# Three constant products of a recurrence: plain float32, or two float32r products of split parts

## The chip, the cores and the metric

The kernel runs on one core of a Trainium2 chip. The metric is the device time of one execution in microseconds; a kernel's time is the median of its runs. A profile of one execution stands beside the times: it gives every instruction's start and length on each engine.

## The reference, cut to what matters

One layer of a hybrid encoder block works on 2048 tokens of width 1024: a combined projection, chunked attention, an RWKV-7 recurrence with 8 heads of 64, a gated merge, and a feed-forward part. The change lies in the recurrence, in what is computed of r, k and v before the scan:

```python
kk = heads(k * k_k)
kk = kk / jnp.maximum(jnp.sqrt(jnp.sum(kk * kk, axis=-1, keepdims=True)), 1e-12)
...
mu = jnp.mean(y, axis=-1, keepdims=True)
yn = (y - mu) * lax.rsqrt(var + GN_EPS)
...
bonus = jnp.sum(r_h * k_h * r_k.astype(jnp.float32), axis=-1, keepdims=True) * v_h
```

Three of its sums run over the 64 channels of a head: the sum of squares of kk, the mean that is taken from the output (the kernel takes it from v ahead of the scan, since the output is linear in v), and the bonus sum.

## The kernel before, in words

The 2048 tokens go through in four groups of 512 (`for g in range(self.NG)` in `run`). In each group `phase_rwkv` handles four pairs of heads (128 channels on the partitions), then `phase_attention` and `phase_merge` follow; after the four groups comes the feed-forward part. `rwkv_pre` (line 418 on) runs once for each pair and group, so 16 times in all. The text calls the four pairs of a group pair 0 to 3. Pairs 0 and 1 are prepared in the open; pairs 2 and 3 are prepared while the matrix inverse and the recurrence of pairs 0 and 1 are under way.

Nearly all of TensorE's work is dense projections. `dense` (line 117) forms a block of 128 output columns for 512 tokens out of 24 products of 128x128 by 128x512: the float32 operands are split into a float32r high part (ScalarE's cast, line 80) and a low part (VectorE's subtraction, line 81), and `mm3` (line 83) issues high by high, high by low and low by high. The tile is called psd. `self.mm` is the last product of the latest dense block.

`rwkv_pre` forms r, k and v of the pair by dense blocks and `mix` (token shift: ScalarE lines 372 and 375, GpSimd's column copies of `carry` lines 373 and 374, VectorE line 376). Then come, all in plain float32 on TensorE:

- sums of squares: sq is k squared on ScalarE (line 461); ps_ss takes four products, sq's 128 tokens as the stationary side and the 128x2 constant bones2 as the moving side (line 464). n2t on VectorE is the inverse (lines 466, 467), and GpSimd spreads it into n2 (line 474).
- centred values: ps_v takes four products of v's 128 tokens with the 128x128 constant cmat (line 516); ScalarE copies them into SV (lines 520, 521).
- bonus: r times r_k times k on VectorE (line 502); ps_bonus is one product of the constant bones with the 128x512 tile r (line 525); VectorE multiplies it by v (line 526) and GpSimd's queue stores it (line 527).

BK (lines 496, 499) holds the decayed keys that ps_bk (line 536) and ps_A (line 557) read. mN (line 505) is a masked copy of n2 that is read when ps_A is moved out (line 573). AR, tk, ta, Ei are further operands of the same pair.

The order on each engine is set by a list scheduler when the kernel is built: it goes by program order and by its own estimates of when inputs are ready. `between()` places a dense block of the output gates, or a piece of the running recurrence, at marked points of `rwkv_pre` (the tables `GATES` and `STEPS`). `tc.issue_after(x)` holds an instruction behind x on its engine. Once built, the order on an engine is fixed: an instruction that isn't ready holds up all behind it. PSUM tiles of tag "a" come from a pool of two buffers; tags "BK" and "mN" have one buffer each.

Of the kernel before, what the change touches and what calls it, by code (L numbers as in the profile page):

```python
# [17 lines left out]
P = 128  # L18
# [5 lines left out]
G = 512  # L24
GT = G // P
C = 64
NC = G // C
# [27 lines left out]
class Block:  # L55
# [109 lines left out]
    def constants(self, ctx, mixing):  # L165
        tc, nc, a = self.tc, self.nc, self.a
        keep = ctx.enter_context(tc.tile_pool(name="const", bufs=1))
        cp = mixing.enter_context(tc.tile_pool(name="mconst", bufs=1, side="right"))
# [4 lines left out]
        self.g2c = keep.tile([P, 2 * KB], F32, name="g2c")  # L173
        self.nhalf = keep.tile([P, 8], F32, name="nhalf")
        nc.vector.memset(self.nhalf, -0.5)
        self.bones = cp.tile([P, P], F32, name="bones")
        nc.vector.memset(self.bones, 0.0)
        for h in range(2):
            nc.vector.memset(self.bones[h * C : h * C + C, h * C : h * C + C], 1.0)
        self.bones2 = cp.tile([P, 2], F32, name="bones2")  # L180
        nc.vector.memset(self.bones2, 0.0)
        for h in range(2):
            nc.vector.memset(self.bones2[h * C : h * C + C, h : h + 1], 1.0)

        self.id64 = cp.tile([P, C], F32, name="id64")
        for h in range(2):
            nc.vector.tensor_copy(self.id64[h * C : h * C + C], self.ident[h * C : h * C + C, h * C : h * C + C])
        self.cmat = cp.tile([P, P], F32, name="cmat")
        nc.vector.scalar_tensor_tensor(
            self.cmat, self.bones, -1.0 / C, self.ident, op0=ALU.mult, op1=ALU.add  # L190
        )
# [30 lines left out]
        with tc.tile_pool(name="setup", bufs=1, side="right") as sp, \  # L222
# [18 lines left out]
            ps = pp.tile([P, nrow], F32, name="ps_rows")  # L241
# [4 lines left out]
            for par in range(2):  # L246
                r = slice(par * C, par * C + C)
# [132 lines left out]
    def tmp(self, name, shape=(P, G)):  # L380
        return self.tp.tile(list(shape), F32, tag="t", name=name)

    def lora_wa(self, g):

        nc, lp = self.nc, self.lp
        rows = [slice(0, C), slice(C, P)]
        lw = self.tmp("lw")
        self.mix(g, 12, lw)
        nc.scalar.activation(lw[0:C], lw[0:C], AF.Tanh)

        self.lo = []
# [27 lines left out]
    def rwkv_pre(self, g, p, rp, NA, between, pools):  # L419
        nc = self.nc  # L420
        pc = slice(p * P, (p + 1) * P)
        col = slice(p, p + 1)
        R = {}
        r = self.tmp("r")
# [3 lines left out]
        ps = self.lora(0, p)  # L428
# [5 lines left out]
        ps = self.lora(1, p)  # L434
        ta = self.tmp("ta")
        nc.scalar.activation(ta, ps, AF.Tanh, scale=0.5, bias=self.ha0[:, col])
        v = self.tmp("v")
# [22 lines left out]
        sq = self.tmp("sq")  # L460
        nc.scalar.activation(sq, k, AF.Square, scale=self.kk[:, col])
        pss = self.pa.tile([P, GT, 2], F32, tag="a", name="ps_ss")
        for t in range(GT):
            nc.tensor.matmul(pss[:, t], sq[:, t * P : (t + 1) * P], self.bones2, start=True, stop=True)
        n2t = self.tp.tile([P, GT, 2], F32, tag="n2t", bufs=2, name="n2t")
        nc.vector.tensor_scalar(n2t, pss, 1e-24, None, ALU.max)
        nc.vector.reciprocal(n2t, n2t)
# [10 lines left out]
        BK = self.tp.tile([P, NC, 2, C], F32, tag="BK", bufs=1, name="BK")  # L478
# [21 lines left out]
        between()  # L500

        nc.vector.scalar_tensor_tensor(r, r, self.rk[:, col], tk, op0=ALU.mult, op1=ALU.mult)
        mN = self.tp.tile([P, 2, NC, C], F32, tag="mN", bufs=1, name="mN")
        for par in range(2):
            nc.vector.tensor_tensor(
# [2 lines left out]
                n2[:, :, par, None].to_broadcast((P, NC, C)),  # L508
                ALU.mult,
            )  # L510
        between()

        SV = rp.tile([P, NC, 2, C], F32, tag="SV", name="SV")
        psv = self.pa.tile([P, GT, P], F32, tag="a", name="ps_v")
        for t in range(GT):
            nc.tensor.matmul(psv[:, t], v[:, t * P : (t + 1) * P], self.cmat, start=True, stop=True)
        SVv = SV.rearrange("p (t h) e c -> p h t e c", h=2)
        for h in range(2):
            src = psv[h * C : h * C + C]
            nc.scalar.copy(SVv[C:P, h, :, 0], src[:, :, 0:C])  # L520
            nc.scalar.copy(SVv[0:C, h, :, 1], src[:, :, C:P])
        R["SV"] = SV

        psb = self.pa.tile([P, G], F32, tag="a", name="ps_bonus")
        nc.tensor.matmul(psb, self.bones, r, start=True, stop=True)
        nc.vector.tensor_tensor(r, psb, v, ALU.mult)
        nc.gpsimd.dma_start(self.bvd[p], r)

        between()

# [104 lines left out]
    def rwkv_trans(self, p, R):  # L635

        nc, xp = self.nc, self.xp
        AR, SV, XT, BR = (R[x] for x in ("AR", "SV", "XT", "BR"))
        rows = [slice(0, C), slice(C, P)]
# [18 lines left out]
        for h, cs in enumerate(halves):  # L658
# [1044 lines left out]
```

## Time and profile before

| what | value |
|---|---|
| time, median of 3 runs | 3239.71 us (3233.46, 3239.71, 3240.22) |
| span of the profiled execution | 3233.6 us, 49175 instructions |
| the same execution's own time | the page prints none; the runs lie 0.1 us below to 6.6 us above its span |
| TensorE products, weight loads | busy 3189.0 us (99%), 2568.5 us (79%) |
| VectorE, ScalarE, GpSimd | 2259.7 us (70%), 1572.6 us (49%), 392.5 us (12%) |
| dense products psd, three kinds | 1344 each, 533 to 542 us busy each |
| recurrence stage of the second group, 500 to 760 us | TensorE busy 256.71 of 260 us |

A matmul's busy time includes its filling and draining, which overlap with the next one's: the cost of a product is read from the distance between starts. A plain float32 product appears in the profile as two records, each with its own weight load, a float32r product as one. A row of the timeline gives the start, the length, the engine (PEld is the weight load), the line, the operation, the tiles as out<-in, the shape, and in brackets the idle time ahead of it and what ended it.

### The profile page before, as it was taken

The numbers are of one execution on the slowest core, as the hardware profiler recorded it, in microseconds if no ns is written. First come the engines' busy times: TensorE is split into PE (matmuls) and PEld (weight loads), VectorE is DVE, ScalarE is ACT, GpSimd is POOL, SyncE is SP. The second block draws the span as 40 slices with busy tenths as digits, with TensorE's granted clock in tenths as the row PEclk, the third lists the DMA queues.
The fourth block names the chain that finished last, engine by engine and source line by source line (L and its number), as shares of the span: only waits on it lengthen the run. The fifth ranks groups of instructions, "written<-read, shape, count | busy, mean of one in ns | idle before, by whom it ended". The sixth has DMA issues, their size and how long they took to land. (4 is left out here: it accounts for less than half of the span.)

```text
span 3233.6 us, 49175 instructions
## 1 busy us (share of the span) xinstructions
PE 3189.0 (99%) x18945; PEld 2568.5 (79%) x18945; DVE 2259.7 (70%) x3782; ACT 1572.6 (49%) x2551; POOL 392.5 (12%) x757
## 2 busy tenths in 40 slices
PE   8999999999999999999999999999999999999999
PEld 6777788777778777778777778878888888888887
DVE  6784556775676774576774666777778988766788
ACT  4435534444655435645434635467543454454333
POOL 2111002111021111022111000033000121100001
PEclk9999999999999999999999999999999999999999
DMA  5224343234264224354224257577546474453443
GB/s 163 91 83 151 105 145 117 73 109 168 94 241 137 79 102 149 110 206 166 85 85 151 92 182 280 185 248 254 185 169 221 161 268 177 175 169 137 158 161 130
DMA packets 166163, 498.34 MB, mean 154 GB/s; under 512 B 18141, under 2 KB 26529, under 8 KB 160553
## 3 DMA queue, kind: packets, MB, share of 16 engines
q1 hardware_dynamic: 107000, 358.33, 33.0%
q0 software_dynamic: 22688, 77.61, 6.3%
q10 hardware_dynamic: 36240, 59.26, 5.0%
q8 instruction: 149, 2.44, 0.3%
q14 instruction: 86, 0.70, 0.1%
HBM read 366.13 MB, written 132.15 MB: 154 GB/s over the span
## 5 line engine op out<-in xcount | busy, mean ns | idle before, releaser
L89 PE MATMUL psd<-hh,wlo 128*128 128x512 f32 x1344 | 534.3, 398 | 10.0 <-DVE wlo L81 10.0
L89 PE MATMUL psd<-hh,whi 128*128 128x512 f32 x1344 | 541.9, 403 | 0.4
L89 PE MATMUL psd<-hl,whi 128*128 128x512 f32 x1344 | 532.8, 396 | 0.0
L80 ACT CAST whi<-wraw 128x1024 fp32r<-128x1024 f32 x232 | 243.7, 1050 | 497.6 <-PE psd L89 355.5
L89 PE MATMUL ps_dn<-fop,fop 128*128 128x512 f32 x2016 | 457.3, 389 | 0.0
L89 PEld LDWEIGHTS ps_dn<-fop,fop 128*128 128x128 f32 x2016 | 378.5, 188 | 78.5
L81 DVE TENSOR_TENSOR wlo<-wraw,whi 128x1024 fp32r<-128x1024 f32 x232 | 282.7, 1220 | 148.5 <-ACT whi L80 147.1
L89 PEld LDWEIGHTS psd<-hh,wlo 128*128 128x128 f32 x1344 | 253.5, 189 | 68.9 <-DVE wlo L81 14.7
L89 PEld LDWEIGHTS psd<-hh,whi 128*128 128x128 f32 x1344 | 253.3, 188 | 57.1 <-issue 2.6
L89 PEld LDWEIGHTS psd<-hl,whi 128*128 128x128 f32 x1344 | 253.7, 189 | 46.3 <-issue 0.7
L80 ACT CAST fop<-ar 128x1024 fp32r<-128x1024 f32 x84 | 87.8, 1050 | 212.2 <-PE ps_dn L89 172.8
L89 PE MATMUL ps_dn<-fop 128*128 128x512 f32 x768 | 175.6, 390 | 0.3 <-DVE fop L81 0.3
L89 PEld LDWEIGHTS ps_dn<-fop 128*128 128x128 f32 x768 | 143.9, 188 | 31.4 <-DVE fop L81 0.7
L1441 DVE TENSOR_TENSOR y<-y,ps_dn 128x512 f32<-128x512 f32 x168 | 109.2, 682 | 43.5 <-PE ps_dn L89 42.7
L81 DVE TENSOR_TENSOR fop<-ar,fop 128x1024 fp32r<-128x1024 f32 x84 | 102.3, 1220 | 45.4 <-ACT fop L80 45.4
L932 DVE CUSTOM_DVE_ANT_0 sc<-bias,ps_s 128x640 f32<-128x640 f32 (+4 forms) x128 | 94.1, 735 | 56.2 <-PE ps_s L926 53.7
L937 ACT ACTIVATE sc<-sc,mn 128x640 f32<-128x640 f32 (+4 forms) x128 | 97.8, 764 | 34.9 <-DVE mn L932 33.1
L1326 POOL DMA_DIRECT2D sd<-slots x96 | 53.0, 552 | 454.1 <-DVE slots L1325 450.2
L1059 PE MATMUL ps_o<-wlo,mh 128*128 128x512 f32 x256 | 101.1, 395 | 3.6 <-DVE wlo L81 3.6
L1059 PE MATMUL ps_o<-whi,mh 128*128 128x512 f32 x256 | 101.5, 400 | 0.5 <-ACT whi L80 0.5
L89 PE MATMUL ps_p<-yh,wlo 128*128 128x512 f32 x256 | 100.9, 394 | 0.0
L1059 PE MATMUL ps_o<-whi,ml 128*128 128x512 f32 x256 | 100.9, 394 | 0.0
(381 smaller groups left out, 6817.8 us busy)
## 6 DMA issues: line engine op xcount, KB each, us to landing
wraw<-in_w_in_dram SPq DMA_DIRECT2D x168, 512.0 KB
ar<-sd SPq DMA_DIRECT2D x42, 1024.0 KB
wraw<-in_w_up_dram SPq DMA_DIRECT2D x82, 512.0 KB
sd<-slots POOLq DMA_DIRECT2D x96, 256.0 KB, 5.0
qb<-in_w_down_dram SPq DMA_DIRECT2D x24, 1024.0 KB
gd<-gate ACTq DMA_DIRECT2D x64, 256.0 KB
wraw<-in_w_out_dram SPq DMA_DIRECT2D x32, 512.0 KB
sd<-slots ACTq DMA_DIRECT2D x60, 256.0 KB
```

The costliest lines, as they stand in the source:

```text
L80: self.cast = self.nc.scalar.copy(hi, src).ins
L81: self.parted = self.nc.vector.tensor_tensor(lo, src, hi.bitcast(F32), ALU.subtract).ins
L89: mm = nc.tensor.matmul(ps, l, r, start=start and n == 0, stop=stop and n == last).ins
L932: nc.vector.tensor_tensor_reduce(sc[:, 0:n], bias[:, s0:640], pss[:, c0 : c0 + n], 1.0, 3.0e38, ALU.add, ALU.min, mn,)
L937: nc.scalar.activation(sc[:, 0:n], sc[:, 0:n], AF.Exp, scale=-1.0, bias=mn, accum_out=sm)
L1059: nc.tensor.matmul(ps[t], l[:, k, ts], r[:, k % 2], start=k == 0 and j == 0, stop=k == KB - 1 and j == 2)
L1326: nc.gpsimd.dma_start(place(i, "s3" if o == "a21" else o), R[o])
L1441: self.add = nc.vector.tensor_tensor(dst, dst, ps, ALU.add).ins
```

## The change

The constants become float32r tiles. They are exact in that form: zeros, ones, and multiples of 1/64. A new helper, `parts`, splits a 128x512 float32 tile into a float32r high part (a ScalarE copy) and a low part (a GpSimd subtraction, which reads the tile and the high part). `by_token` issues, for each of the four blocks of 128 tokens, the low part's product and then the high part's, accumulated in PSUM. The three sums are taken this way: ps_ss and ps_v by `by_token`, ps_bonus by two products of 128x512. Each of these products is held behind `self.mm`.

No memory is added: the parts of sq use the buffer of BK, and the parts of v, then those of r, use the buffer of mN. So BK is now written after ps_ss has read the parts, parts of r come after ps_v, and mN is formed after the bonus. The two `between()` calls near the bonus keep their count: one moves ahead of ps_v and mN moves behind the bonus.

```diff
@@ -173,19 +173,18 @@
-        self.bones = cp.tile([P, P], F32, name="bones")
+        self.sums = cp.tile([P, P], F32R, name="sums")
+        self.bones = self.sums.bitcast(F32)
...
-        self.bones2 = cp.tile([P, 2], F32, name="bones2")
-        nc.vector.memset(self.bones2, 0.0)
-        for h in range(2):
-            nc.vector.memset(self.bones2[h * C : h * C + C, h : h + 1], 1.0)
+        self.sums2 = cp.tile([P, 2], F32R, name="sums2")
+        nc.vector.tensor_copy(self.sums2, self.bones[:, 0 : 2 * C : C])
...
-        self.cmat = cp.tile([P, P], F32, name="cmat")
+        self.cmat = cp.tile([P, P], F32R, name="cmat")
@@ -380,6 +379,20 @@
+    def parts(self, src, tag):
+
+        both = self.tp.tile([P, 2, G], F32R, tag=tag, bufs=1, name="parts")
+        self.nc.scalar.copy(both[:, 0], src)
+        self.nc.gpsimd.tensor_tensor(both[:, 1], src, both[:, 0].bitcast(F32), ALU.subtract)
+        return both
+
+    def by_token(self, ps, both, mat):
+
+        for t in range(GT):
+            for i in (1, 0):
+                with self.tied(self.mm):
+                    self.nc.tensor.matmul(ps[:, t], both[:, i, t * P : (t + 1) * P], mat, start=i == 1, stop=i == 0)
+
@@ -460,8 +473,7 @@
         sq = self.tmp("sq")
         nc.scalar.activation(sq, k, AF.Square, scale=self.kk[:, col])
         pss = self.pa.tile([P, GT, 2], F32, tag="a", name="ps_ss")
-        for t in range(GT):
-            nc.tensor.matmul(pss[:, t], sq[:, t * P : (t + 1) * P], self.bones2, start=True, stop=True)
+        self.by_token(pss, self.parts(sq, "BK"), self.sums2)
@@ -500,6 +512,25 @@
         nc.vector.scalar_tensor_tensor(r, r, self.rk[:, col], tk, op0=ALU.mult, op1=ALU.mult)
+        between()
+
+        SV = rp.tile([P, NC, 2, C], F32, tag="SV", name="SV")
+        psv = self.pa.tile([P, GT, P], F32, tag="a", name="ps_v")
+        self.by_token(psv, self.parts(v, "mN"), self.cmat)
...
+        psb = self.pa.tile([P, G], F32, tag="a", name="ps_bonus")
+        both = self.parts(r, "mN")
+        for i in (1, 0):
+            with self.tied(self.mm):
+                nc.tensor.matmul(psb, self.sums, both[:, i], start=i == 1, stop=i == 0)
+        nc.vector.tensor_tensor(r, psb, v, ALU.mult)
+        nc.gpsimd.dma_start(self.bvd[p], r)
         mN = self.tp.tile([P, 2, NC, C], F32, tag="mN", bufs=1, name="mN")
         for par in range(2):
...
-        between()
-
-        SV = rp.tile([P, NC, 2, C], F32, tag="SV", name="SV")
-        psv = self.pa.tile([P, GT, P], F32, tag="a", name="ps_v")
-        for t in range(GT):
-            nc.tensor.matmul(psv[:, t], v[:, t * P : (t + 1) * P], self.cmat, start=True, stop=True)
...
-        psb = self.pa.tile([P, G], F32, tag="a", name="ps_bonus")
-        nc.tensor.matmul(psb, self.bones, r, start=True, stop=True)
-        nc.vector.tensor_tensor(r, psb, v, ALU.mult)
-        nc.gpsimd.dma_start(self.bvd[p], r)
```

The places below are all in the second group; the other groups have the same order there. First TensorE in pair 1, at the sums of squares, before. The names: ps_ss and ps_v as above, psd the dense block of the next gate.

```order
L89 MATMUL psd<-hl,whi 128x512
L464 MATMUL ps_ss<-bones_104,sq 128x2 x4
L516 MATMUL ps_v<-cmat,v 128x128 x4
L89 MATMUL psd<-hh,wlo 128x512
L89 MATMUL psd<-hh,whi 128x512
L89 MATMUL psd<-hl,whi 128x512
```

The same place after the change.

```order
L89 MATMUL psd<-hh,whi 128x512
L394 MATMUL ps_ss<-sums_104,parts 128x2 x8
L89 MATMUL psd<-hl,whi 128x512
L89 MATMUL psd<-hh,wlo 128x512
L394 MATMUL ps_v<-cmat,parts 128x128 x8
L571 MATMUL ps_A<-AR,BK 128x128 x4
L89 MATMUL psd<-hh,whi 128x512
L89 MATMUL psd<-hl,whi 128x512
L571 MATMUL ps_A<-AR,BK 128x128 x4
L89 MATMUL psd<-hh,wlo 128x512
L531 MATMUL ps_bonus<-parts,sums 128x512 x2
```

Each of the two products has eight instructions in place of four, the dense block that ended with v's is followed by 22 dense products ahead of ps_ss instead of 14, two of the ten that stood between ps_v and ps_A now stand ahead of ps_v, and none stands between ps_v and ps_A.

Then VectorE in pair 1, before: tk, ta and BK are the operands of the keys, n2t the inverse of the sums of squares.

```order
L466 TENSOR_SCALAR n2t<-ps_ss 128x8
L467 RECIPROCAL n2t<-n2t 128x8
L489 TENSOR_TENSOR tk<-tk,k 128x512
L490 SCALAR_TENSOR_TENSOR ta<-ta,k 128x512
L499 TENSOR_TENSOR BK<-tk,Ei 64x8x64
L496 SCALAR_TENSOR_TENSOR BK<-ta,hkk,Ei 64x8x64 x2
L499 TENSOR_TENSOR BK<-tk,Ei 64x8x64
L502 SCALAR_TENSOR_TENSOR r<-r,cst,tk 128x512
L505 TENSOR_TENSOR mN<-mI,n_5425 128x512 x2
```

And after:

```order
L501 TENSOR_TENSOR tk<-tk,k 128x512
L502 SCALAR_TENSOR_TENSOR ta<-ta,k 128x512
L514 SCALAR_TENSOR_TENSOR r<-r,cst,tk 128x512
L478 TENSOR_SCALAR n2t<-ps_ss 128x8
L508 SCALAR_TENSOR_TENSOR BK<-ta,hkk,Ei 64x8x64
L479 RECIPROCAL n2t<-n2t 128x8
L511 TENSOR_TENSOR BK<-tk,Ei 64x8x64
L508 SCALAR_TENSOR_TENSOR BK<-ta,hkk,Ei 64x8x64
L511 TENSOR_TENSOR BK<-tk,Ei 64x8x64
```

tk, ta and r now stand ahead of n2t, which waits for ps_ss; BK follows n2t directly, and mN has left this place.

Last TensorE in pair 2, at the centred values and the bonus, before: ps_ug, ps_tq and ps_y are products of the running recurrence.

```order
L663 MATMUL ps_ug<-WA,XT 64x128 x16
L691 MATMUL ps_y<-SV,BR 64x64
L516 MATMUL ps_v<-cmat,v 128x128 x4
L525 MATMUL ps_bonus<-r,bones 128x512
L691 MATMUL ps_y<-SV,BR 64x64 x6
L674 MATMUL ps_tq<-BR,GT 64x128 x16
```

And after:

```order
L677 MATMUL ps_ug<-WA,XT 64x128 x16
L705 MATMUL ps_y<-SV,BR 64x64
L394 MATMUL ps_v<-cmat,parts 128x128 x8
L705 MATMUL ps_y<-SV,BR 64x64 x15
L89 MATMUL psd<-hl,whi 128x512
L89 MATMUL psd<-hh,wlo 128x512
L89 MATMUL psd<-hh,whi 128x512
L89 MATMUL psd<-hl,whi 128x512
L89 MATMUL psd<-hh,wlo 128x512
L89 MATMUL psd<-hh,whi 128x512
L531 MATMUL ps_bonus<-parts,sums 128x512 x2
```

The bonus stood right behind ps_v; now the rest of ps_y and six dense products lie between them. On GpSimd the three subtractions of a pair stand in this order: sq, v, then the four copies of n2, then r, then the store of line 527 (now 533).

More of the change, by code (lines that the diff above doesn't have):

```diff
@@ L502, in rwkv_pre @@
         nc.vector.scalar_tensor_tensor(r, r, self.rk[:, col], tk, op0=ALU.mult, op1=ALU.mult)
+        between()
+        SV = rp.tile([P, NC, 2, C], F32, tag="SV", name="SV")
+        psv = self.pa.tile([P, GT, P], F32, tag="a", name="ps_v")
+        self.by_token(psv, self.parts(v, "mN"), self.cmat)
+        SVv = SV.rearrange("p (t h) e c -> p h t e c", h=2)
+        for h in range(2):
+            src = psv[h * C : h * C + C]
+            nc.scalar.copy(SVv[C:P, h, :, 0], src[:, :, 0:C])
+            nc.scalar.copy(SVv[0:C, h, :, 1], src[:, :, C:P])
+        R["SV"] = SV
+        psb = self.pa.tile([P, G], F32, tag="a", name="ps_bonus")
[5 more added lines that the diff above has]
+        nc.gpsimd.dma_start(self.bvd[p], r)
         mN = self.tp.tile([P, 2, NC, C], F32, tag="mN", bufs=1, name="mN")
@@ L510, in rwkv_pre @@
             )
-        between()
-        SV = rp.tile([P, NC, 2, C], F32, tag="SV", name="SV")
-        psv = self.pa.tile([P, GT, P], F32, tag="a", name="ps_v")
-        for t in range(GT):
[L516 to L522, printed above, removed]
-        psb = self.pa.tile([P, G], F32, tag="a", name="ps_bonus")
-        nc.tensor.matmul(psb, self.bones, r, start=True, stop=True)
-        nc.vector.tensor_tensor(r, psb, v, ALU.mult)
-        nc.gpsimd.dma_start(self.bvd[p], r)
         between()
```

## Prediction

> **What bounds the kernel now.** I read the page first, then busy time by stretches, then the groups by form, then the timeline around the four pairs of the second group. The page and the stretch of that group's recurrence:
>
> ```profile
> PE 3189.0 (99%) x18945; PEld 2568.5 (79%) x18945; DVE 2259.7 (70%) x3782; ACT 1572.6 (49%) x2551; POOL 392.5 (12%) x757
> core 0: us, PE busy (x) PEld busy (x) DVE busy (x) ACT busy (x) POOL busy (x), PEclk, DMA share, GB/s
> 500.00:760.00 260.00, 256.71 (x2168) 204.95 (x2167) 178.66 (x383) 113.36 (x195) 37.05 (x66) 0.99 0.28 95
> ```
>
> TensorE is the bound in the recurrence too: 3.3 of 260 us idle, at full clock. So a microsecond of TensorE saved or lost there is one of the kernel. The three products by form:
>
> ```profile
> L516 PE MATMUL ps_v<-cmat,v 128*128 128x128 f32 x128 | 18.4, 286 | 0.2
> L525 PE MATMUL ps_bonus<-r,bones 128*128 128x512 f32 x32 | 17.5, 627 | 0.0
> L464 PE MATMUL ps_ss<-bones,sq 128*128 128x2 f32 x128 | 16.4, 250 | 0.3 <-ACT sq L461 0.3
> ```
>
> They cost little, and TensorE hardly waits for their operands (0.3 and 0.2 us in 16 pairs). Pair 0, with what follows and what feeds it:
>
> ```profile
> 514.08 0.72 ACT L461 ACTIVATE sq<-k,cst 128x512 f32<-128x512 f32 x1
> 514.70 0.81 ACT L488 ACTIVATE tk<-ta,c,hka 128x512 f32<-128x512 f32 x1
> 515.54 0.69 DVE L489 TENSOR_TENSOR tk<-tk,k 128x512 f32<-128x512 f32 x1 [0.65 <-ACT tk L488]
> 517.02 0.95 PE L464 MATMUL ps_ss<-bones,sq 128*128 128x2 f32 x8
> 517.84 1.14 PE L516 MATMUL ps_v<-cmat,v 128*128 128x128 f32 x8
> 518.73 0.48 PE L89 MATMUL psd<-hh,whi 128*128 128x512 f32 x1
> 519.01 2.15 POOL L474 COPY n<-n2t 64x4 f32<-64x4 f32 x4 [3.81 <-DVE n2t L467]
> 519.01 0.37 ACT L520 COPY SV<-ps_v 64x256 f32<-64x256 f32 x1 [0.39 <-PE ps_v L516]
> 519.05 0.39 PE L89 MATMUL psd<-hl,whi 128*128 128x512 f32 x1
> 519.28 0.39 PE L89 MATMUL psd<-hh,wlo 128*128 128x512 f32 x1
> 520.20 0.37 ACT L521 COPY SV<-ps_v 64x256 f32<-64x256 f32 x1
> 520.86 0.39 PE L89 MATMUL psd<-hh,whi 128*128 128x512 f32 x1
> 521.25 1.10 PE L525 MATMUL ps_bonus<-r,bones 128*128 128x512 f32 x2
> ```
>
> From start to start: ps_ss 0.82 us, ps_v 0.89, a dense product 0.23 (0.32 right after ps_v). ps_ss starts 2.2 us after sq is done.
>
> **TensorE's own work.** An undisturbed bonus, in pair 3, with the next product:
>
> ```profile
> 659.39 1.02 PE L525 MATMUL ps_bonus<-r,bones 128*128 128x512 f32 x2
> 660.25 0.49 PE L536 MATMUL ps_bk<-ident,BK 128*128 128x128 f32 x3
> ```
>
> It takes 0.86 us. Two float32r products of this shape take 2 x 0.23 = 0.46, as dense products do: 0.40 saved, times 16 = **6.4 us**. For the narrow products the attention has float32r ones of 128 columns, between dense products:
>
> ```profile
> 304.78 0.40 PE L89 MATMUL psd<-hh,wlo 128*128 128x512 f32 x1
> 305.01 0.23 PE L926 MATMUL ps_s<-KK,QA 128*128 128x128 f32 x1
> 305.07 0.27 PE L926 MATMUL ps_s<-KK,QB 128*128 128x128 f32 x1
> 305.19 0.45 PE L89 MATMUL psd<-hh,whi 128*128 128x512 f32 x1
> ```
>
> The pair takes 0.18, or 0.09 each. Eight plain records take 0.82 and 0.89, or 0.10 to 0.11 each. By these rows eight float32r products with eight weight loads cost the same to 0.2 us less; I take the same, since each still loads a new 128x128 block.
>
> **The low part's price.** Each pair gains three ScalarE casts of 128x512 (0.62 us by the row below) and three GpSimd subtractions. GpSimd has no two-input operation of this size. Its rows nearest to it:
>
> ```profile
> L80 ACT CAST s4h<-s 128x512 fp32r<-128x512 f32 x32 | 19.9, 623 | 13.3 <-PE ps_u L89 11.8 <-ACT slots L1314 1.6
> L606 POOL MEMSET XT<- 32x512 f32 x16 | 8.3, 519 | 14.1 <-PE ps_ug L663 13.4
> L470 POOL MEMSET n<- 128x16 f32 x16 | 1.5, 111 | 44.9 <-DVE NA L566 40.3 <-DVE x L344 4.4
> L226 POOL TENSOR_SCALAR_AFFINE_SELECT eye<-eye 2x512 f32<-2x512 f32 x1 | 0.8, 842 | 0.1
> ```
>
> Writing 512 elements takes 0.52 us, reading and writing them 0.84. One more stream of 512 at the memsets' slope, (519-111)/(512-16) = 0.82 ns each, adds 0.42: 1.26. So 0.52 is the floor, 0.84 the low end with one input read, 1.26 the upper end, and I take the middle of the last two, 1.05 us, since a second input is read but may overlap. [...]
>
> GpSimd also waits for VectorE:
>
> ```profile
> 512.64 1.22 DVE L81 TENSOR_TENSOR wlo<-wraw,whi 128x1024 fp32r<-128x1024 f32 x1 [2.48 <-ACT whi L80]
> 513.22 0.69 POOL L374 COPY carry<-pr 128x1 f32<-128x1 f32 x1 [2.88 <-ACT pr L372]
> 515.02 0.18 POOL L373 COPY pr<-carry 128x1 f32<-128x1 f32 x1 [1.11 <-DVE v L376]
> ```
>
> A one-column copy takes 0.18 us with VectorE idle and 0.69 here, where it ends 0.05 us after the VectorE subtraction beside it (513.86). So I let each GpSimd subtraction wait for the VectorE operation that is running.
>
> **Where the low parts are late.** The added wait stands on TensorE: all dense products queue behind it. 0.1 us is allowed for each handover.
>
> Pair 0: TensorE arrives at 517.02. The cast of sq follows tk at 515.4 and ends at 516.0; tk on VectorE runs to 516.23; the low part is there at 516.25+1.05+0.1 = 517.4: wait 0.4. The low part of v follows at once, but r now runs on VectorE until 517.5, so it is there at 518.65, where ps_ss has ended at 518.2: wait 0.4. Call the end of ps_v V. SV is copied out from V+0.3 to V+1.85 (the rows from 519.01 to 520.57), the cast of r ends at V+2.4, GpSimd has the copies of n2 (2.15 us) ahead of it, and with half a VectorE operation (0.35) the low part of r is there at V+4.0. TensorE has 12 dense products: V+2.8. Wait 1.2. Together 2.0.
>
> Pair 1:
>
> ```profile
> 548.39 0.72 ACT L461 ACTIVATE sq<-k,cst 128x512 f32<-128x512 f32 x1
> 549.00 0.81 ACT L488 ACTIVATE tk<-ta,c,hka 128x512 f32<-128x512 f32 x1
> 549.16 1.05 PE L464 MATMUL ps_ss<-bones,sq 128*128 128x2 f32 x8
> ```
>
> Fourteen dense products (0.227 each) lie between v's dense block and ps_ss, and TensorE waits 0.1 us for sq, so that block ends at 549.16-0.1-3.2 = 545.9. Now 22 products stand there: TensorE arrives at 545.9+22x0.227 = 550.9. The cast ends at 550.3, VectorE's tk at 550.64, the low part comes at 551.8: wait 0.9. ps_ss ends at S = 552.6; the two dense products cover the low part of v. But ps_A now follows ps_v directly, at S+1.35, and needs two of the four BK, which stand behind n2t: 0.15 of handover, two short operations of 0.2 and two like tk on VectorE (0.69), so S+1.9: wait 0.6. The bonus gets its low part 0.6 late by the same steps as in pair 0. Together 2.1.
>
> Pair 2: sq and v are early. The products ps_y of the recurrence, before:
>
> ```profile
> 616.49 0.97 PE L691 MATMUL ps_y<-SV,BR 128*64 128x64 f32 x25
> ```
>
> Thirteen products, two records each, take about 0.86 us and 0.11 of draining. After ps_v stand 15 ps_y (0.06 each, 0.9) and six dense products (1.45): V+2.35. The low part of r comes after SV (1.65), the cast (0.6), 1.05 and handovers: V+3.55, with VectorE idle. Wait 1.2.
>
> Pair 3, with the last product of its v block, which so ends at 648.7:
>
> ```profile
> 648.48 0.39 PE L89 MATMUL psd<-hh,wlo 128*128 128x512 f32 x1
> 651.26 0.72 ACT L461 ACTIVATE sq<-k,cst 128x512 f32<-128x512 f32 x1
> 651.87 0.81 ACT L488 ACTIVATE tk<-ta,c,hka 128x512 f32<-128x512 f32 x1
> 653.12 1.05 PE L464 MATMUL ps_ss<-bones,sq 128*128 128x2 f32 x8
> ```
>
> Before, nine dense products and six steps of the recurrence lie between (4.4 us, so 0.39 a step); now 13 and seven: TensorE arrives at 654.4, the low part at 654.65: wait 0.2. For the bonus, r stands on VectorE behind n2t, ta and four BK: six operations like tk (0.69), two short ones, 4.5 us after ps_ss ends at 655.5; cast, subtraction and handovers make it 661.95 against TensorE's 660.6: wait 1.35. Together 1.55.
>
> A group loses 2.0+2.1+1.2+1.55 = 6.85 us, less 0.25 that ps_ss and the bonus wait now: 6.6, times 4 = 26.4. Less 6.4 saved: **+20 us**. The ScalarE casts (48 x 0.62 = 30 us) have no other price: ScalarE is busy 49%. mN behind the bonus and BK behind ps_ss are in the sum where TensorE waits for them. The profiled span becomes 3233.6+20 = 3253.6; the median of the runs lies 6.1 us above that span, so I forecast 3239.7+20 = **3260 us**. With 0.84 and no wait for VectorE the same steps give 3.65 a group: +8.
>
> **The rivals.** *The low parts are in time: faster.* It decides where a subtraction takes well under 0.5 us, or where ScalarE's casts run ahead of what I laid out. Then only the bonus and the present waits change: -6.4-1.0 = -7.4, 3232. For it: ps_ss in pair 0 has 2.2 us of room. Against it: GpSimd needs 0.52 us to write alone.
>
> *The floor: no change.* At 0.52 us per subtraction, with no wait for VectorE, the same steps leave 2.4 a group, mostly where VectorE is late with BK or r: 9.6-6.4 = +3, 3243.
>
> *The lock works both ways: slower still.* If VectorE's two-input operations also stop for the whole GpSimd subtraction, each of some eight waits a group grows by about one VectorE operation (0.7) or subtraction: 12.6 a group, 50-6 = +44, 3284. The rows show GpSimd behind VectorE and no VectorE operation behind GpSimd. [...]
>
> *The products don't get cheaper.* If the bonus kept its 0.86 us, the result would be +26, 3266.
>
> **How the numbers follow.** Forecast 0.50, both-ways lock 0.12, no cheaper product 0.04: slower by over 0.2% 0.66. The floor case: within 0.2% 0.16. In time: faster 0.18. 0.2% (6.5 us) is about what a measurement of this kernel can tell from no change. The range reaches from the faster rival, 3232, to the lock, 3284. The likeliest sign's own range is 3247 to 3284.
>
> **What would show it.** After the change the timeline should show two ps_bonus products 0.23 apart, GpSimd subtractions near 1.05 us, longer beside VectorE, and TensorE idle ahead of ps_ss, ps_v and ps_bonus, released by GpSimd: some 0.4 to 1.3 us each, largest at the bonus, none at ps_ss of pair 2. TensorE's idle time from 500 to 760 us should grow by about 6 us. I am wrong if the subtractions take about 0.5 us, or if these idle times are missing.

## The result, and the profile after

The changed kernel takes 3283.47 us (median of 4 runs, 3279.6 to 3289.19); the kernel before takes 3238.0 us (median of 4 runs, 3233.46 to 3240.22; the three of the table ahead of the prediction and one more of 3236.29). The ratio is 1.0144, with a 95% interval of 1.013 to 1.0157: slower, as forecast, but by 45.5 us and not by 20.

The profiled execution of the changed kernel took 3279.6 us, its span is 3277.9. First its page's row of engines and the stretch of the second group's recurrence, then the three products by form:

```profile
PE 3208.0 (98%) x18945; PEld 2584.7 (79%) x18945; DVE 2288.3 (70%) x3780; ACT 1598.2 (49%) x2599; POOL 462.0 (14%) x805
```

```profile
core 0: us, PE busy (x) PEld busy (x) DVE busy (x) ACT busy (x) POOL busy (x), PEclk, DMA share, GB/s
500.00:760.00 260.00, 252.50 (x2078) 202.77 (x2076) 181.69 (x371) 117.29 (x202) 52.52 (x80) 0.97 0.28 87
```

```profile
L394 PE MATMUL ps_v<-cmat,parts 128*128 128x128 f32 x128 | 18.2, 287 | 3.1 <-POOL parts L386 2.5
...
L394 PE MATMUL ps_ss<-sums,parts 128*128 128x2 f32 x128 | 16.4, 250 | 3.9 <-POOL parts L386 3.9
...
L531 PE MATMUL ps_bonus<-parts,sums 128*128 128x512 f32 x32 | 13.0, 491 | 8.2 <-POOL parts L386 8.2
```

Two things happened to TensorE. Its idle time, span less busy time, went from 3233.6 - 3189.0 = 44.6 us to 3277.9 - 3208.0 = 69.9 us. And its busy time grew by 19.0 us, though the bonus got cheaper (17.5 to 13.0 us busy). The second shows in the column PEclk: 0.97 in this stretch, where it was 0.99. Pair 0 of the second group in the timeline, with all three engines that the low parts concern:

```profile
522.93 0.61 ACT L385 CAST parts<-sq 128x512 fp32r<-128x512 f32 x1
...
523.62 1.29 POOL L386 TENSOR_TENSOR parts<-sq,parts 128x512 fp32r<-128x512 f32 x1 [1.26 <-ACT parts L385]
...
523.68 1.79 DVE L502 SCALAR_TENSOR_TENSOR ta<-ta,k 128x512 f32<-128x512 f32 x1
...
524.87 1.72 POOL L386 TENSOR_TENSOR parts<-v,parts 128x512 fp32r<-128x512 f32 x1
...
524.97 1.05 PE L394 MATMUL ps_ss<-sums,parts 128*128 128x2 f32 x8 [0.26 <-POOL parts L386]
525.39 1.75 DVE L514 SCALAR_TENSOR_TENSOR r<-r,cst,tk 128x512 f32<-128x512 f32 x1
...
526.64 1.87 PE L394 MATMUL ps_v<-cmat,parts 128*128 128x128 f32 x8 [0.62 <-POOL parts L386]
...
528.31 0.73 PE L89 MATMUL psd<-hh,whi 128*128 128x512 f32 x1
...
528.84 0.63 PE L89 MATMUL psd<-hl,whi 128*128 128x512 f32 x1
...
529.27 0.63 PE L89 MATMUL psd<-hh,wlo 128*128 128x512 f32 x1
```

Read the starts of the dense products: 528.84 and 529.27 lie 0.43 us apart, where before they lay 0.23 apart. TensorE runs at half speed here, and nothing that the product waits for says so. Five stretches of 3.413 us around this place, cut where the clock changes, show it:

```profile
519.98:523.39 3.41, 3.41 (x16) 2.82 (x15) 2.21 (x3) 3.41 (x7) 0.87 (x2) 1.00 0.31 56
523.39:526.80 3.41, 2.53 (x15) 1.88 (x14) 3.41 (x3) 2.31 (x4) 2.96 (x2) 1.00 0.24 97
526.80:530.22 3.42, 3.42 (x13) 3.03 (x14) 3.37 (x8) 1.64 (x5) 2.05 (x4) 0.50 0.20 77
530.22:533.63 3.41, 3.41 (x10) 2.64 (x9) 0.94 (x1) 0.35 (x1) 2.28 (x2) 0.50 0.40 114
533.63:537.04 3.41, 3.41 (x20) 2.63 (x19) 2.73 (x5) 0.00 (x0) 0.62 (x1) 1.00 0.27 109
```

The second has TensorE busy for 2.53 of 3.41 us, at full clock: the two waits, 0.26 and 0.62, are the rest. The next two are at 0.50 although TensorE has work all the time. So a short wait was followed by 6.83 us at half clock. The trace also records the granted clock itself; added up between 50 and 3190 us, the half-clock stretches are 6.8 us before (two, of 3.413 us each) and 68.3 us after (thirteen, each a multiple of 3.413 us). The mean clocks of the two profiled runs agree with that: 0.998 before and 0.989 after. It is no accident of one execution: the four runs of the changed kernel have mean clocks of 0.985 to 0.990, the 50 runs of the kernel before that were made beside the experiments 0.996 to 0.999.

One of the two stretches before lies in the row from 500 to 760 us that the prediction shows, and its 0.99 is that stretch. It too follows a short wait, here for the low part of a weight:

```profile
708.59 0.50 PE L89 MATMUL psd<-hh,wlo 128*128 128x512 f32 x1 [1.38 <-DVE wlo L81]
```

```profile
709.20:712.60 3.40, 3.40 (x10) 2.25 (x9) 0.47 (x1) 1.37 (x3) 0.00 (x0) 0.50 0.90 282
```

From here on a span is read as three parts: idle time of TensorE; what half clock costs, which I estimate as half of the half-clock time, since the granted clock is 0.50 there; and work, which is TensorE's busy time less that half. Before: 44.6 + 3.4 + 3185.6. After: 69.9 + 34.2 + 3173.9. The difference of 44.3 us is then **+25.3 idle, +30.8 half clock, -11.7 work.** The split is not exact, since the work does not take twice as long at half clock (dense products stand 0.43 us apart, less than twice the 0.23): among kernels with the same products, the work of the experiments below agrees to within 8 us.

Last the groups by form of the subtractions and of the two VectorE operations beside them, ta and r, and what TensorE waits for. First ta and r before (the line numbers are 12 lower there):

```profile
L502 DVE SCALAR_TENSOR_TENSOR r<-r,cst,tk 128x512 f32<-128x512 f32 x16 | 12.0, 751 | 0.3
...
L490 DVE SCALAR_TENSOR_TENSOR ta<-ta,k 128x512 f32<-128x512 f32 x16 | 10.8, 672 | 0.0
```

And after:

```profile
L386 POOL TENSOR_TENSOR parts<-v,parts 128x512 fp32r<-128x512 f32 x16 | 27.5, 1718 | 0.0
...
L514 DVE SCALAR_TENSOR_TENSOR r<-r,cst,tk 128x512 f32<-128x512 f32 x16 | 24.1, 1508 | 0.1
...
L386 POOL TENSOR_TENSOR parts<-sq,parts 128x512 fp32r<-128x512 f32 x16 | 22.8, 1424 | 20.8 <-ACT parts L385 20.8
...
L502 DVE SCALAR_TENSOR_TENSOR ta<-ta,k 128x512 f32<-128x512 f32 x16 | 20.9, 1306 | 0.0
...
L386 POOL TENSOR_TENSOR parts<-r,parts 128x512 fp32r<-128x512 f32 x16 | 20.3, 1271 | 18.2 <-ACT parts L385 9.7 <-issue 6.2 <-POOL n L486 2.0
```

```profile
PE ps_bonus L531 <- POOL parts L386: 8.2, 11, 2.0
...
PE ps_st L716 <- DVE ST L719: 3.9, 4, 1.0
PE ps_ss L394 <- POOL parts L386: 3.9, 8, 0.7
PE ps_A L571 <- DVE BK L511: 3.7, 4, 0.9
...
PE ps_v L394 <- POOL parts L386: 2.5, 4, 0.6
```

A subtraction takes 1.27 us alone (that of r). In pair 0, ta starts 0.06 us after the subtraction of sq and takes 1.79 us; the subtraction of v then starts inside ta and takes 1.72; r starts inside that and takes 1.75. Each of these three ends a little under one undisturbed duration after the one before it (ta 0.56 us after, undisturbed 0.67; the subtraction of v 1.12, undisturbed 1.27; r 0.55, undisturbed 0.75): GpSimd and VectorE take turns here, in both directions. Over all 16 pairs, ta grew from 0.67 to 1.31 us on average and r from 0.75 to 1.51.

### The profile page after: what moved, and what is told of

Read it like the earlier page. It is cut to its first block, busy times and chain, and to the rows that moved or that the text cites. A ratio compares the mean times of both kernels' runs of the same rounds, so it can differ in the third digit from the quotient of the medians.

```text
span 3277.9 us, 49274 instructions
## 1 busy us (share of the span) xinstructions
PE 3208.0 (98%) x18945; PEld 2584.7 (79%) x18945; DVE 2288.3 (70%) x3780; ACT 1598.2 (49%) x2599; POOL 462.0 (14%) x805
## 5 line engine op out<-in xcount | busy, mean ns | idle before, releaser
L89 PE MATMUL psd<-hl,whi 128*128 128x512 f32 x1344 | 539.4, 401 | 0.0
```

What stands on the lines that cost most here:

```text
L89: mm = nc.tensor.matmul(ps, l, r, start=start and n == 0, stop=stop and n == last).ins
```

## Experiments

Theory A: TensorE stands for late low parts, and these short stands bring the half clock. Theory B: waits and the lock between VectorE and GpSimd alone; the clock only goes along. Theory C: the split products and their tied place cost the time. All kernels in one table. Each ratio is to runs of the kernel before that were made beside that kernel (their medians lie from 3236.3 to 3238.3 us). The four columns behind it are of one profiled execution, in us, with the parts of the span as above. The mean clock of the other runs of a kernel differs by 0.001 to 0.006, and 0.001 stands for some 6.5 us at half clock (an estimate: 3240 x 0.001 / 0.5), so differences of 10 to 20 us in that column are not safe by themselves.

```
kernel                 median   ratio to before (95%)    span    idle  half clock  work
before                 3238.0                            3233.6  44.6   6.8        3185.6
after                  3283.5   1.0144 (1.0130-1.0157)   3277.9  69.9  68.3        3173.9
low part on VectorE    3250.2   1.0040 (1.0024-1.0056)   3249.7  60.8  37.5        3170.1
filled                 3275.7   1.0119 (1.0103-1.0136)   3274.9  51.3  13.7        3216.8
high part only         3214.0   0.9935 (0.9914-0.9956)   3213.2  55.3  13.7        3151.1
bonus only             3243.9   1.0018 (1.0007-1.0029)   3240.9  53.5  20.5        3177.2
narrow only            3270.0   1.0096 (1.0081-1.0111)   3263.9  58.8  47.8        3181.2
low part unread        3261.8   1.0067 (1.0050-1.0084)   3264.5  83.5  64.9        3148.6
high part first        3271.9   1.0104 (1.0089-1.0119)   3268.5  65.2  51.2        3177.7
waits alone            3279.8   1.0130 (1.0115-1.0145)   3278.5  73.1  47.8        3181.5
bonus early, VectorE   3249.5   1.0039 (1.0026-1.0052)   3247.8  54.3  23.9        3181.6
source freed           3237.3   1.0007 (0.9996-1.0018)   3230.8  68.8  20.5        3151.8
narrow filled          3277.5   1.0129 (1.0115-1.0142)   3276.6  61.9  23.9        3202.8
bonus early, GpSimd    3241.1   1.0004 (0.9995-1.0013)   3241.6  55.4  20.5        3176.0
```

**The gaps filled.** Of all runs this one separates the theories most.

```diff
-    def by_token(self, ps, both, mat):
...
+    def by_token(self, ps, both, mat, full):
...
+        for _ in range(4):
+            with self.tied(self.mm):
+                self.nc.tensor.matmul(full, self.sums, both[:, 0], start=True, stop=True)
```

(`full` is the 512 columns of the same PSUM buffer; a loop like this, which writes psb, stands ahead of the bonus.)

> The changed kernel, and ahead of each of its three groups of split products four more 128x512 products of the high part, whose result is overwritten: 16 x 3 x 4 x 0.227 = 43.6 us of added TensorE work that needs the cast only, so that it stands where TensorE now waits for the low part. The output is unchanged. Theory A: most of the 25 us of idle time is filled, half-clock time falls from 65 us to under 25 us, which gives back some 20 us: 3275 to 3292 us, so the added work is nearly free. Theory B: only the idle time is filled and the half clock stays: 3284 + 43.6 - 20 = 3300 to 3312 us. Theory C: 3284 + 43.6 = 3320 us or more.

Measured 3275.69 us, with a mean clock of 0.997 to 0.998 in its four runs. The page's row of engines:

```profile
PE 3223.6 (98%) x19137; PEld 2599.8 (79%) x19137; DVE 2284.3 (70%) x3780; ACT 1597.4 (49%) x2599; POOL 457.1 (14%) x805
```

TensorE has 192 more products, and the kernel is 7.8 us faster than the changed one. The work is 3216.8 us, and less 43.6 for the filling it is 3173.2, against 3173.9 of the changed kernel: the parts add up. The added work was paid for by 18.6 us of idle time and, more than that, by 27.3 us of half clock: 54.6 us less of it. The low parts, the lock and the products of the change are all still there, so B and C fall as the whole cause.

**The gaps at the narrow products filled only.** The same four lines in `by_token`, none at the bonus.

> The changed kernel with the four filling products of the high part ahead of the sums of squares and of the centred values only: 16 x 2 x 4 x 0.227 = 29.1 us of added TensorE work, and nothing filled at the bonus. The output is unchanged. In the traces so far a stretch of half clock follows a 3.41 us window in which the idle time and 0.45 of the time of narrow products together pass about 1.7 us. By that rule the windows at ps_ss and ps_v (48 of 68 us of half clock) go and those behind the bonus and in the recurrence stay: 18 to 35 us of half clock, 3275 to 3290 us. If any filled microsecond counts the same wherever it stands, the half-clock time falls by two thirds of 54 us, to about 32. Theory B (the clock is a bystander): 68 us of half clock stay and the time is 3300 us or more.

Measured 3277.48 us with 23.9 us at half clock. With two thirds of the filling, 44 of the 68 us are gone, four fifths of what the whole filling removes. Both are within what was expected. The column doesn't decide between the rule and the rival that every filled microsecond counts the same (some 32 us): the four runs' mean clocks, 0.995 to 0.998, span more than that difference. Of the six stretches that are left, three stand where the whole filling also leaves one (near 94, 1080 and 1587 us of the span). The work agrees once more: 3202.8 - 29.1 = 3173.7.

**Waits without split products.**

```diff
-        self.nc.scalar.copy(both[:, 0], src)
-        self.nc.gpsimd.tensor_tensor(both[:, 1], src, both[:, 0].bitcast(F32), ALU.subtract)
+        self.nc.scalar.activation(both[:, 0], src, AF.Copy, scale=0.0)
+        self.nc.gpsimd.tensor_tensor(both[:, 1], src, both[:, 0], ALU.add)
```

(with a plain float32 tile for `both`, and one plain fp32 product of `both[:, 1]` in place of each two.)

> The changed kernel's ScalarE and GpSimd operations and its places of the products, but without split products: ScalarE makes zeros in place of the high part, GpSimd adds them to the source, and the plain fp32 products of the kernel before read that sum. The output is unchanged. Theory A: the late operands alone bring the loss: TensorE's work is 5 to 6 us more than in the changed kernel, the waits and the half-clock time (50 to 80 us) the same: 3280 to 3296 us. Theory C: without split products the loss goes: 3240 to 3260 us.

Measured 3279.77 us. TensorE's waits for GpSimd:

```profile
PE ps_bonus L529 <- POOL parts L386: 15.1, 14, 1.7
...
PE ps_ss L393 <- POOL parts L386: 3.9, 8, 0.7
...
PE ps_v L393 <- POOL parts L386: 2.5, 4, 0.6
```

Those ahead of ps_ss and ps_v are to the tenth those of the changed kernel, and the loss is there without any split product: theory C falls. The time lies at the lower edge of A's range. Its parts differ from those of the changed kernel: 3.2 us more idle time, 20.5 us less half clock (47.8, a little less than I expected), and 7.6 us more work.

**The parts of the change apart.** The bonus split alone, and the narrow products split alone; the others are plain fp32 as before.

```diff
-        self.by_token(pss, self.parts(sq, "BK"), self.sums2)
+        for t in range(GT):
+            nc.tensor.matmul(pss[:, t], sq[:, t * P : (t + 1) * P], self.sums2.bitcast(F32), start=True, stop=True)
...
```

> The changed kernel with the sums of squares and the centred values as plain fp32 products again, so that the bonus alone is split. Theory A: about half of the late parts stay (11.9 of 24.4 us of waits of weight loads for GpSimd are the bonus's), and with them about half of the half-clock time; 12 us of waits + 13 of half clock - 6.4 saved: 3250 to 3264 us. Theory B: 12 - 6.4: 3240 to 3250 us. Theory C (the products): the bonus is cheaper as predicted and only the narrow products cost: 3228 to 3236 us.

> The changed kernel with the bonus as one plain fp32 product again, so that the sums of squares and the centred values alone are split. Theory A (late low parts, and the half clock that they bring): the splits of the narrow products carry most of the half-clock time, since the bonus alone had 20 us of it and the whole change 68; the waits ahead of ps_ss and ps_v stay (6 us), those of ps_A (4 us) too: 3262 to 3278 us with 35 to 60 us at half clock. Theory B (waits and the lock alone): 3238 + 10 = 3245 to 3254 us. Theory C (the split narrow products cost it by themselves): 3275 to 3290 us, with no more half clock than before.

Measured 3243.85 and 3270.04 us. The bonus alone costs less than theory A said, and the time lies in B's range: its idle time is 8.9 us more than before, but half clock only 13.7 us more. The narrow products bring 14.2 us more idle time and 41.0 us more half clock, in A's range of time and of half clock. So half clock doesn't go with idle time alone; where the wait stands counts. The ten runs of the kernel with the bonus alone show the clock's weight by themselves: two at a mean clock of 0.998 took 3235.58 and 3237.1 us, and seven at 0.995 and 0.996 took 3242.44 to 3249.01.

**The low part on VectorE.** `self.nc.vector.tensor_tensor` in place of `self.nc.gpsimd.tensor_tensor`.

> The changed kernel, but the low part is subtracted on VectorE (about 0.7 us, the length of its other 128x512 operations) and not on GpSimd (1.27 alone, 1.72 beside VectorE). Theory A (TensorE stands about 25 us more for late low parts, and these stands also bring some 58 us more at half clock): the low parts come 0.6 to 1.0 us sooner and the lock is gone, so idle time and half-clock time both fall by more than half: 3240 to 3258 us. Theory B (waits and the lock alone, the clock is a bystander): 3240 to 3255 us, with the half-clock time as in the changed kernel. Theory C (the split products and their fixed place cost the time, whoever makes the low part): 3272 to 3290 us.

Measured 3250.17 us, with TensorE waiting for a low part only at the bonus, 3.1 us in all. A and B both expected this time. Half clock falls from 68.3 to 37.5 us, where B had it unchanged; but neither it nor the idle time falls by more than half, as A had it. VectorE's 48 added operations make other things late: TensorE now waits 15.6 us for the matrix inverse on VectorE, which it didn't before. The six stretches of half clock begin behind windows with 2.0 to 3.0 us of idle time.

**High parts first.** The eight products of the high part ahead of the eight of the low part, and the same at the bonus.

> The changed kernel with the products of the high part first and those of the low part behind them (eight and eight, one and one at the bonus). The work is the same, but the low part may come 0.4 us (narrow) or 0.23 us (bonus) later. Theory A: waits ahead of ps_ss nearly go, those ahead of ps_v and the bonus shrink, and half-clock time falls by more than a third: 3255 to 3275 us. Theory B: 48 x 0.2 to 0.3 us sooner at most: 3270 to 3278 us with the half-clock time unchanged. Theory C: 3280 us or more.

Measured 3271.9 us; 4.7 us less idle time and 17.1 us less half clock than in the changed kernel. It lies within A's range and within B's, and both missed in part: the waits ahead of ps_ss nearly went (3.9 to 0.7 us), but those at ps_v and the bonus grew (2.5 to 4.6 and 8.2 to 11.7), and half clock fell by a quarter, not by more than a third.

**The low part left out, made unread, and made without being in the way.**

```diff
-            for i in (1, 0):
+            for i in (0,):
```

> The changed kernel without low parts: no subtraction on GpSimd and one float32r product of the high part in place of two, so it leaves the low part out of the three sums. The place and the tie of the products stay. TensorE has some 24 us less work than in the kernel before (0.63 of 0.86 us in 16 bonus products, about half of 16 x 1.71 us in the narrow ones). Theories A and B: no late parts, so 3212 to 3230 us, with half-clock time near the 7 us of before under A. Theory C: the place of the products costs it, 3250 us or more.

> The kernel with high parts only (3214 us), and the GpSimd subtractions of the changed kernel beside it, whose result no product reads; the low part is so left out of the three sums. VectorE stops for GpSimd as in the changed kernel, but TensorE waits for no low part. Theory A: 3214 to 3226 us with less than 30 us at half clock. Theory B (the lock, through VectorE's later operations, costs most): 3236 to 3256 us.

> The kernel with high parts only (3214 us), and 48 GpSimd subtractions of the same size beside it that read the high part alone and write where no later instruction waits for them soon (tw, which is dead by then); so the low part is left out of the three sums. GpSimd and VectorE still stop each other, but r, BK and mN no longer stand behind the subtractions, as they do in the kernel whose low part was made and not read (3262 us). If the lock itself costs much: 3240 us or more. If the low part's place in the chain of buffers (r is overwritten, BK and mN use its buffer) was the cost there: 3214 to 3226 us.

The first gave 3214.02 us, as expected, so place and tie of the products can't be what costs 45 us. They may cost something: its idle time is 10.7 us above that of before. The second was a miss for both theories: 3261.83 us, 47.8 us more, for low parts that no product reads. What TensorE waits for there, and what VectorE waits for:

```profile
PE ps_bk L550 <- DVE r L532: 9.9, 10, 2.0
...
PE ps_A L571 <- DVE BK L511: 7.3, 4, 1.8
...
PE ps_bk L550 <- DVE BK L511: 5.1, 4, 1.3
```

```profile
DVE r L532 <- POOL parts L386: 35.0, 14, 6.2
...
DVE BK L508 <- POOL parts L386: 1.9, 4, 0.5
```

The wait has moved one step down the pair. BK is written over the buffer of sq's parts, and `r = psb * v` overwrites the r that GpSimd still reads, so VectorE stands behind the subtraction, and TensorE behind VectorE. The third kernel ("source freed" in the table) subtracts the high part from itself, into tw: 3237.34 us. It lies between its two expectations, nearer to that of the lock. It frees r, for which VectorE no longer waits. It doesn't free BK and mN, though its expectation says so: the subtraction still reads the high part, which lies in their buffers, and VectorE still waits 3.3 us for it there, where the kernel with high parts alone has no such wait:

```profile
L387 POOL TENSOR_TENSOR tw<-parts 128x512 f32<-128x512 f32 x48 | 60.7, 1265 | 36.8 <-ACT parts L385 35.2
```

```profile
PE ps_A L572 <- DVE BK L512: 5.3, 4, 1.3
...
PE ps_bk L551 <- DVE BK L512: 3.1, 4, 0.8
...
PE ps_bk L551 <- DVE r L533: 2.7, 4, 0.7
```

```profile
DVE mN L537 <- POOL tw L387: 2.4, 4, 0.6
DVE BK L509 <- POOL tw L387: 0.9, 4, 0.3
```

Idle time is 13.5 us more than with high parts alone, nearly all behind VectorE. By the medians the place of r was about half of the 47.8 us. The other half, 23.3 us over the high parts alone (17.6 us between the two profiled spans), belongs to the lock together with what is left of the waits for buffers; no run has the lock by itself.

**Towards a better version.** The bonus alone split, its parts made right behind r, the high part's product first, and the low part on VectorE or on GpSimd.

> The bonus alone is split, its low part is subtracted on VectorE, both parts are made right behind r and ahead of the centred values, and the product of the high part goes first; the rest is as in the kernel before. Theory A: no late low part, so idle time and half clock stay as before and only the cheaper bonus is left: 3238 - 6 = 3229 to 3236 us. Against it: the cast and the subtraction now stand ahead of SV's copies and of later work on VectorE, and if a wait of over 1.5 us comes from that, half clock comes with it: 3236 to 3246 us. Theory C: the tied place costs: 3244 us or more.

> As the kernel with the bonus alone split and its parts made early (3249.5 us), but with the low part on GpSimd as in the change. VectorE so gets no work more, and stops for GpSimd in 16 subtractions instead. If the loss there came from VectorE's 16 added subtractions, which made later weight parts late for TensorE (waits for wlo 13.6 us before, 22.3 there): the waits for wlo go back to about 14 us, half clock to under 15 us, and the cheaper bonus shows: 3230 to 3239 us. If VectorE's stops for GpSimd count the same (16 x 1.0 us): 3242 to 3252 us, with more than 20 us at half clock. Late low parts should not show in either case: no wait of the bonus for GpSimd.

Measured 3249.52 and 3241.13 us. Neither beats the kernel before; the second can't be told from it. The first lies above A's range and in the range of theory C, but the second, with the same places and ties, lies below that range, so the place alone doesn't explain the first. With the low part on VectorE no bonus waits for it, but the weight parts are later. TensorE's waits for them, before and there:

```profile
PE psd L89 <- DVE wlo L81: 10.0, 8, 1.7
...
PE ps_o L1059 <- DVE wlo L81: 3.6, 4, 1.3
```

```profile
PE psd L89 <- DVE wlo L81: 15.5, 8, 2.4
...
PE ps_o L1075 <- DVE wlo L81: 6.8, 5, 2.5
```

These waits are 8.7 us more than before, and half clock is 17 us more. With the low part on GpSimd they are 17.1 us in place of 22.3, so some 5 us of them go with VectorE's sixteen operations of 0.7 us. The rest is not explained: the kernel with high parts alone, which adds nothing to VectorE, has 20.4 us. The second time lies between its two expectations, and its half clock of 20.5 us fits the one in which VectorE's stops for GpSimd count as much. The bonus waits for GpSimd eight times all the same, which I had excluded:

```profile
PE psd L89 <- DVE wlo L81: 9.6, 5, 2.0
PE ps_o L1075 <- DVE wlo L81: 7.5, 4, 3.4
PE ps_bonus L533 <- POOL parts L386: 4.9, 8, 0.8
```

## Why the prediction was wrong in size

*TensorE is the bound.* Right: with the span read as idle time, work and half of the half-clock time, kernels with the same products have the same work to within 8 us.

*The bonus saves 0.40 us each, 6.4 in all.* Nearly. From the start of the bonus to the start of the next product it took 0.95 us on average over 16 before and takes 0.61 where it alone is split: 0.34, or 5.4 us. It isn't 0.46 us after the change, as I had it, since the product behind the second one starts later. After, in pair 2:

```profile
644.24 0.73 PE L531 MATMUL ps_bonus<-parts,sums 128*128 128x512 f32 x2 [0.84 <-POOL parts L386]
644.90 0.76 PE L688 MATMUL ps_tq<-BR,GT 64*64 64x128 f32 x10
```

*The narrow products cost the same.* Right: from its start to that of the next product, ps_ss takes 0.92, 0.98 and 0.88 us in pairs 1 to 3 of the second group after the change, and 0.91, 0.98 and 0.98 before. The work of the changed kernel is 3 us below that of the bonus alone, less than the 8 us to which work agrees.

*A subtraction takes 1.05 us.* Too low: 1.27 alone, just above the upper end of 1.26, as if the second input didn't overlap at all. The floor rival (0.52 us) and the rival that all low parts are in time are refuted by this row.

*GpSimd waits for the running VectorE operation, and not the other way.* Wrong in its second half, and I had given the other case 0.12. VectorE waits too: in pair 0 ta takes 1.79 us, and before the change it took 0.67 on average. GpSimd does wait, as I had it: the subtraction of v, which starts inside ta, takes 1.72 us against 1.27 alone. The rival that waits both ways named 3284 us, the measured time, but that is luck: it had the waits of TensorE for the low parts nearly double, and they came out below the forecast, and half clock had no part in it.

*The waits, 27.4 us a kernel.* By the rows above, ps_ss waits 3.9 us (6.0 forecast), ps_v 2.5 (1.6), ps_A 3.7 (2.4), the bonus 8.2 (17.4): 18.3 in all. The bonus's waits were over-rated. In the pair shown above the bonus waits not at all, since the dense products ahead of it run at half clock, from 526.8 to 533.6, and give GpSimd the time. The idle time as a whole still grew by 25.3 us against 26.4 forecast; this agreement is partly luck, since 7 us of it stand in later places that VectorE's delays reach (ps_st 3.9 us).

*The sum.* Idle time and work together give +13.6 us, and the forecast +20 would have been 6 us too high. **The step that failed is the one that was not there: 30.8 us of half clock.** The prediction read "at full clock" off the row from 500 to 760 us, though its 0.99 holds the stretch of half clock at 709 us that follows a wait of 1.38 us, carried it over to a kernel with more gaps, and priced a wait at its own length ("a microsecond of TensorE saved or lost there is one of the kernel"). Its cases and ranges all held that price. Its signs of being wrong held nothing on the clock either: the subtractions took more than 0.5 us and the idle times ahead of the three sums were there, so none of these signs came up.

*What sets the half clock off.* I cut the spans of all 14 profiled runs, from 45 to 1950 us, into the 3.413 us windows in which the clock changes, and took those at full clock, 7681 in number; 85 are followed by one at half clock. By TensorE's idle time in the window itself, from its records:

```
idle in the window, us     under 0.3  0.3-0.6  0.6-0.9  0.9-1.2  1.2-1.6  1.6-2.0  over 2.0
windows                         7202      178      119       64       64       27        27
followed by half clock             0        2       13        6       21       16        27
```

Between 0.6 and 1.6 us of idle time it is the narrow products (all with under 512 columns) that go with half clock; their time is counted where no wide one runs. With under 0.5 us of them in the window 1 of 125 is followed by half clock, with 0.5 to 1.5 us 18 of 85, with 1.5 to 2.5 us 21 of 36. The line that parts the cases best is idle + 0.45 x narrow = 1.74 us, about half of the window; 34 of the 7681 fall on the wrong side, against 51 with the best limit on idle time alone. The line is a fit to these traces, and a rough one: of the 13 stretches of the changed kernel, six begin behind a window under the line. The pair shown above is one of them, since its 0.88 us of idle time and 1.2 us of narrow products make 1.42. The rule stood in the expectation of one run, the narrow gaps filled. It fits that the waits ahead of ps_ss and ps_v are the dear ones: in the windows there that half clock follows, 0.6 to 1.0 us of idle time stand beside 1.2 to 2.0 us of narrow products, while the bonus's waits, mostly 0.5 to 0.8 us, stand among wide ones.

What stays open: how the cost parts between late low parts and lock in the changed kernel, since the subtractions that no product reads and that leave r free (23.3 us over the high parts) and the late parts lie partly on the same microseconds, and no run has the lock by itself. And that the clock reacts to little activity, and not to something that goes with it in these windows, was shown for filled gaps only; no run made a gap of chosen length among wide products.

## What to carry to other kernels

Where TensorE is busy 99% of the time, a wait of it can cost more than its own length (here 25.3 us more idle time came with a cost of 30.8 us by half clock): look at the clock in the window behind it. A mean clock of 0.99 is not full clock. Lay any product that is ready into such waits: here 43.6 us of useless products made the changed kernel 7.8 us faster. The fit suggests counting narrow products beside a wait as half idle, and so keeping waits apart from them; no run tried that. And before handing such a subtraction (128x512, two inputs) to GpSimd, count the VectorE operations beside it that it can stop (ta took 1.79 us in place of 0.67), and the buffers that it keeps from being written again.

## What the hardware showed unexpectedly

- Short waits of TensorE can bring half clock: a 3.413 us window at full clock was followed by it in 40 of 247 cases with 0.6 to 1.6 us of idle time, in 43 of 54 with more, and in none of 7202 with under 0.3. In the changed kernel it lasts 3.4 to 10.2 us, and dense products then stand 0.43 us apart in place of 0.23.
- A GpSimd subtraction of 128x512 float32 takes 1.27 us alone. Two VectorE operations that started during one took longer: ta 1.79 us, where it took 0.67 before, and r 1.75, where it took 0.75. The subtraction of v, which started during ta, took 1.72.
- 48 such subtractions whose result no product reads cost 23 us over the kernel without them; where VectorE overwrites their source later, 48 us.
